# More block products by seven multiplications in the second SwiGLU of a streaming-encoder block

## The chip, the cores and the metric

The kernel runs on one core of a Trainium2 chip, as one launch. The metric is the device time of the whole launch in microseconds, the median over runs. Beside it stands one profiled execution, recorded by the hardware profiler; its span is the time from the first to the last recorded instruction.

## The reference

One residual block over 256 tokens of width 2048 in float32, with three sublayers, each followed by a layer norm:

```
x <- LN1(alpha*x + 1/2 * g1 * SwiGLU_1(mod1(x)))
x <- LN2(alpha*x +       g2 * W_out[ mLSTM(u) || RG-LRU(u) ])
x <- LN3(alpha*x + 1/2 * g3 * SwiGLU_2(mod3(x)))

def _swiglu(u, w13, w2):
    g, v = jnp.split(u @ w13, 2, axis=-1)
    return (jax.nn.silu(g) * v) @ w2
```

`mod(x)` is a layer norm without gain, times (1 + scale), plus shift. Shift, scale and gate of each sublayer are columns of `silu(c) @ w_ada + b_ada` (adaLN), a product of a 2048 x 18432 matrix with one vector. `w13` is 2048 x 11264 (gate columns, then value columns, 5632 each) and `w2` is 5632 x 2048. The change is in the third sublayer, SwiGLU_2.

## The kernel before

**Arithmetic.** A float32 weight tile of 128 x 2048 (1 MB) is loaded from DRAM into a `raw` buffer by a DMA of SyncE's queue. `split` (lines 101 to 111) turns it into two float32r tiles: ScalarE (ACT) casts it to `hi` (L108), and VectorE (DVE) subtracts to get `lo` (L110). A product is then three matmuls per 128 x 128 step: activation-high times hi, activation-high times lo, activation-low times hi. `mov_t` (L292 to L294 for work that the planner may move, L133 for work in the order written) does four such steps for one half t of the tokens: 12 matmuls of 128 x 512, called a block product here. `mov_w` does it for both token halves, 24 matmuls for one weight tile.

**The feed-forward stage.** The 5632 hidden columns are 11 blocks (0 to 10) of 512. A block needs eight `w13` tiles: gate and value columns, each with four row groups of 512 input rows. Block 0 begins inside the boundary of the sublayer before it. `rows_block` computes a block in the plain way: 8 tiles, 16 block products. `swiglu` multiplies silu(gate) by value, `turn_one` transposes the result on TensorE, and `w2` tiles multiply it, two blocks at a time, into four 512-column outputs `py`, which DVE adds to `yacc`.

**Seven products.** For blocks 2 to 9 (`FAST`), `fast_block` treats the first 1024 input rows as a 2 x 2 problem: two token halves by two row groups, times two row groups by gate and value columns. It takes seven block products in place of eight, from sums of activations (made once by `sums`, L688 to L703, and kept in `ws`, which takes the room of x) and from sums of weight tiles, made by DVE in place: `ta = tc - ta`, `ta = td - ta`, `tc = td - tc`, `tb = tb - ta` (L756, L761, L766, L775). Each sum is split like a loaded tile. The last 1024 rows (the second quad) are computed in the plain way, eight block products. Between the products stand four `w2` tiles of the two blocks before (`x_tile`).

**Order.** The framework has a planner: it lays the instructions out on each engine's in-order queue by a model of their durations, earlier program order first, and each instruction waits for the buffers and results that it needs. Work issued through the names T, V, A, G, Q keeps its written order. Tiles with one tag share a fixed number of buffers: four `raw`, three `hi`, three `lo`, two `row`, six `slot`, eight PSUM banks. A load waits in SyncE's queue until its buffer is free.

**adaLN tiles.** `tick`, called at each weight load, adds a rate to a credit, and for each whole credit an adaLN tile is loaded into a `raw` buffer too and multiplied and summed by DVE (L210). `FFN2_RATE` is 0.5 in the whole third sublayer, from a credit of -2.

**x.** `sums` stores x (2 MB) to DRAM (`xd`) by POOL's queue before its room is used. After block 9 `restore` loads it again, and ACT multiplies it by alpha. Then DVE multiplies `yacc` by the gate and adds it to x, eight pieces of 128 x 512 (L334, L335). Block 10 follows by `rows_block`, and `closing` does the `w2` products of blocks 8, 9 and 10 and the last layer norm.

Of the kernel before, what the change touches and what calls it, by code (L numbers as in the profile page):

```python
# [16 lines left out]
P = 128  # L17
D = 2048
# [23 lines left out]
FFN2_RATE = 0.5  # L42
# [3 lines left out]
FAST = range(2, 10)  # L46


class Held:
# [4 lines left out]
    def __getitem__(self, key):  # L54
        return self.tile[key]
# [3 lines left out]
def block_kernel(ctx: ExitStack, tc: tile.TileContext, a: dict, out: bass.AP):  # L59
# [594 lines left out]
    def ffn(s, w13, w2, start, following=None):  # L654
# [8 lines left out]
        b0 = RAMP // 4 if start else 0  # L663
# [5 lines left out]
        def rows_block(b, passed=None):  # L669

            i = 8 * (b - b0)
            if passed:
                pg, pv = passed[0], met(passed, w13[4:8], f"fv{s}")
            else:
                pg = [bank(f"fg{s}{b}{t}") for t in range(NT)]
                for k in range(4):
                    end = mov_w(pg, load_w(w13[i + k], f"fg{s}_{b}{k}"), uh, ul, k * 4, k == 0, k == 3)
                    if k in (1, 2):
                        turn_one(end)
                pv = [bank(f"fv{s}{b}{t}") for t in range(NT)]  # L680
                for k in range(4):
                    mov_w(pv, load_w(w13[i + 4 + k], f"fv{s}_{b}{k}"), uh, ul, k * 4, k == 0, k == 3)
# [5 lines left out]
        def sums():  # L688

            nc.gpsimd.dma_start(xd, x.tile)  # L690
            f = raw_tile("sums").rearrange("p (a b) -> p a b", b=P)
            for t in range(NT):
                tk = slice(t * P, (t + 1) * P)
                nc.vector.tensor_add(f[:, 8 * t:8 * t + 8, :], uh[:, 0:8, tk].bitcast(F32), ul[:, 0:8, tk].bitcast(F32))
            a11, a12, a21, a22 = (f[:, 4 * i:4 * i + 4, :] for i in range(4))
            nc.vector.tensor_add(a22, a21, a22)
            nc.vector.tensor_sub(a21, a11, a21)
            nc.vector.tensor_sub(a11, a22, a11)
            nc.vector.tensor_sub(a12, a12, a11)
            both = big.tile([P, 2, KT, P], F32R, tag="x", name="ws")  # L700
            nc.scalar.copy(both[:, 0], f)
            nc.vector.tensor_sub(both[:, 1], f, both[:, 0].bitcast(F32))
# [856 lines left out]
```

## Time and profile before

| | |
|---|---|
| median of 3 runs | 1883.22 us (1880.55 to 1883.65) |
| the profiled execution's own time | 1882.46 us |
| its span | 1880.7 us |
| TensorE busy | 1861.4 us, 99% of the span, 8495 matmuls |
| DVE busy | 1561.3 us, 83% |
| ACT busy | 895.1 us, 48% |
| POOL busy | 43.2 us, 2% |
| read from HBM, written | 514.46 MB, 4.22 MB |
| block 2's first product ends, block 9's first product ends | about 1246.6 us, about 1700.9 us |

A line of grouped instructions gives the kernel's line, the engine, the operation, what it writes and reads, the count, the busy time with the mean of one in nanoseconds, and the idle time ahead of it with what ended it. A timeline line gives start and duration in microseconds, then the instruction, and in brackets the engine's idle time before it and who ended it. Matmuls are pipelined: each shows some 390 ns, and what one costs is seen from the distance of their starts. POOL's queue is that of GpSimd.

### The profile page before, as it was taken

How to read it: one execution, taken by the hardware profiler on the slowest of the kernel's cores; microseconds unless marked ns; L12 is line 12 of the kernel's file. 1: busy time of each engine (PE TensorE's matmuls, PEld its weight loads, DVE VectorE, ACT ScalarE, POOL GpSimd, SP SyncE). 2: the span in 40 equal slices, each digit the busy share in tenths (PEclk: the TensorE clock that was granted, in tenths of full speed). 3: DMA queues.
4: the chain of work that ended last, by engine and by line, in shares of the span. 5: the costliest groups of instructions: out<-in, count | busy, mean ns of one | idle time of the engine just before them, and what ended most of it. 6: DMA issues, size and time to landing. Idle time of an engine off the chain costs nothing.

```text
span 1880.7 us, 21240 instructions
## 1 busy us (share of the span) xinstructions
PE 1861.4 (99%) x8495; PEld 1526.0 (81%) x8495; DVE 1561.3 (83%) x1467; ACT 895.1 (48%) x847; POOL 43.2 (2%) x68
## 2 busy tenths in 40 slices
PE   8999999999999999999999999999999999999998
PEld 5788888888888888788888887878778888888886
DVE  6899998887887987889997877789887788778776
ACT  4543444533334335756644356454544455545441
POOL 0000000000000000100000121000000000000000
PEclk9999999999999999999999999999999999999999
DMA  9989889999899987478687574768855654564662
GB/s 377 417 354 366 319 311 347 357 348 355 344 357 355 339 331 269 148 276 296 244 317 296 203 264 182 268 246 300 307 210 190 224 212 168 202 224 186 239 224 90
DMA packets 74931, 520.06 MB, mean 277 GB/s; under 512 B 8736, under 2 KB 8912, under 8 KB 13520
## 3 DMA queue, kind: packets, MB, share of 16 engines
q1 hardware_dynamic: 72144, 507.54, 71.6%
q0 software_dynamic: 960, 7.37, 1.0%
q10 hardware_dynamic: 1728, 3.80, 0.6%
q8 instruction: 66, 1.08, 0.2%
q14 instruction: 33, 0.27, 0.0%
HBM read 514.46 MB, written 4.22 MB: 276 GB/s over the span
## 4 chain that ended last, share of the span: by engine, by line
PE 92%; DVE 4%; DMA 2%; issue 1%; ACT 1%; POOL 0%; POOLq 0%; DVEq 0%; SPq 0%; ACTq 0%
PE py L133 9%; PE pj L281 5%; PE fa L133 5%; PE fb L133 4%; PE fc L133 3%; PE fd L133 3%; PE py L293 3%; PE py L294 3%; PE py L292 3%; PE pj L283 3%; PE fg L293 3%; PE fg L294 3%; PE fg L292 3%; PE fv L293 3%; PE fv L292 3%; PE fv L294 3%
## 5 line engine op out<-in xcount | busy, mean ns | idle before, releaser
L210 DVE CUSTOM_DVE_ANT_0 ada<-ada,scb,badac 128x2048 f32<-128x2048 f32 x110 | 258.0, 2345 | 39.5 <-DMA ada<-in_w_ada 39.0
L108 ACT CAST hw<-rw 128x2048 fp32r<-128x2048 f32 x81 | 155.1, 1914 | 218.0 <-DMA rw<-in_w 60.6
L110 DVE TENSOR_TENSOR lw<-rw,hw 128x2048 fp32r<-128x2048 f32 x81 | 185.1, 2287 | 55.8 <-ACT hw L108 55.0
L110 DVE TENSOR_TENSOR lfw<-rfw,hfw 128x2048 fp32r<-128x2048 f32 x48 | 109.9, 2289 | 17.2 <-ACT hfw L108 17.2
L281 PE MATMUL pj<-u,hs 128*128 128x512 f32 x512 | 122.5, 391 | 0.0
L108 ACT CAST hra<-rra 128x2048 fp32r<-128x2048 f32 x38 | 72.6, 1914 | 102.2 <-DMA rra<-in_w_r 43.1
L108 ACT CAST hfw<-rfw 128x2048 fp32r<-128x2048 f32 x48 | 91.9, 1915 | 47.8 <-PE py L133 28.2
L281 PEld LDWEIGHTS pj<-u,hs 128*128 128x128 f32 x512 | 94.3, 188 | 18.4
L133 PE MATMUL py<-lw,hth 128*128 128x512 f32 x256 | 99.8, 390 | 2.1 <-DVE lw L110 2.1
L133 PE MATMUL py<-hw,hth 128*128 128x512 f32 x256 | 100.4, 392 | 0.0
L293 PE MATMUL py<-lw,hth 128*128 128x512 f32 x256 | 99.8, 390 | 0.1
L294 PE MATMUL py<-hw,htl 128*128 128x512 f32 x256 | 99.7, 390 | 0.0
L133 PE MATMUL py<-hw,htl 128*128 128x512 f32 x256 | 99.7, 389 | 0.0
L292 PE MATMUL py<-hw,hth 128*128 128x512 f32 x256 | 97.3, 392 | 0.0
L108 ACT CAST hfg<-rfg 128x2048 fp32r<-128x2048 f32 x28 | 53.6, 1914 | 86.1 <-DMA rfg<-in_w 48.8
L108 ACT CAST hs<-rs 128x2048 fp32r<-128x2048 f32 x32 | 61.0, 1908 | 68.7 <-PE pj L281 53.6
L293 PE MATMUL fg<-lfg,u 128*128 128x512 f32 x224 | 87.4, 390 | 0.1
L294 PE MATMUL fg<-hfg,u 128*128 128x512 f32 x224 | 87.3, 390 | 0.0
L293 PE MATMUL fv<-lfv,u 128*128 128x512 f32 x224 | 87.2, 389 | 0.0
L294 PE MATMUL fv<-hfv,u 128*128 128x512 f32 x224 | 87.1, 389 | 0.0
L108 ACT CAST hfv<-rfv 128x2048 fp32r<-128x2048 f32 x28 | 53.6, 1913 | 66.7 <-DMA rfv<-in_w 41.3
L292 PE MATMUL fg<-hfg,u 128*128 128x512 f32 x224 | 84.5, 392 | 0.0
(727 smaller groups left out, 4764.4 us busy)
## 6 DMA issues: line engine op xcount, KB each, us to landing
ada<-in_w_ada SPq DMA_DIRECT2D x138, 1024.0 KB, 6.5
rw<-in_w SPq DMA_DIRECT2D x81, 1024.0 KB, 5.5
rfw<-in_w SPq DMA_DIRECT2D x50, 1024.0 KB, 4.8
rra<-in_w_r SPq DMA_DIRECT2D x45, 1024.0 KB, 7.4
rs<-in_w_s SPq DMA_DIRECT2D x32, 1024.0 KB, 5.0
rfg<-in_w SPq DMA_DIRECT2D x28, 1024.0 KB, 6.7
rfv<-in_w SPq DMA_DIRECT2D x28, 1024.0 KB, 5.5
rwo<-in_w_out SPq DMA_DIRECT2D x16, 1024.0 KB, 4.8
```

The lines of the kernel that those rows point to most:

```text
L108: act.copy(cut(hi, w), like(raw[:, w], hi))
L110: low.tensor_sub(cut(lo, w), like(raw[:, w], lo), cut(hi, w).bitcast(F32))
L133: self.last = getattr(self.engine, op)(*args, **kw)
L210: vec.tensor_tensor_reduce(raw[:, c], raw[:, c], scb[:, c], 1.0, base, ALU.mult, ALU.add, to)
L281: nc.tensor.matmul(ps, hi[:, k * P:(k + 1) * P], both(k), start=k == 0, stop=False)
L283: nc.tensor.matmul(ps[:, 0:S], lo[:, k * P:(k + 1) * P], uh[:, k, :], start=False, stop=k == KT - 1)
L292: pe.matmul(o, acth[:, k0 + j, tk], cut(hi, w), start=first and j == 0, stop=False, **kw)
L293: pe.matmul(o, acth[:, k0 + j, tk], cut(lo, w), start=False, stop=False, **kw)
L294: end = pe.matmul(o, actl[:, k0 + j, tk], cut(hi, w), start=False, stop=last and j == 3, **kw)
```

## The change

The third sublayer gets a function of its own, `last_ffn`. Block 0 and 1 are computed as before.

- Block 10 takes its first quad in seven products too. The `w2` products of blocks 8 and 9 with the first 512 output columns, which stood in `closing`, are placed inside it.
- Blocks 4, 6 and 8 (`DOUBLE`) take both quads in seven products each (plan `D6`); six `w2` tiles stand between them. The blocks after them (5, 7, 9) take one quad (plan `S2`), with two `w2` tiles. Blocks 2 and 3 keep the old order (`S4`).
- In blocks 4, 6, 8 two of the four weight sums of each quad are made by a DMA on POOL's queue that adds a weight tile from DRAM to the tile in SBUF: `c += d` and `a += b`. In other blocks DVE adds them. Signs are changed so that these are additions.
- The activation sums of the second quad are made once, at block 4, into one `slot` and one `row` buffer.
- x is multiplied by alpha and stored right after block 0. After block 9, DVE multiplies `yacc` by the gate in place, and a DMA on POOL's queue adds the stored x to it; `yacc` takes the place of x from there.
- The transposed result of a block lies in one `slot` buffer of its own, in place of two for two blocks. The row buffer for the tile `c` is no longer used.
- The adaLN rate is 0.8 per load in blocks 0 and 1 and 0.3 after, from a credit of 0; what is left is done at block 4.

```diff
-FFN2_RATE = 0.5
+FFN2_RATE = (0.8, 0.3)
...
-FAST = range(2, 10)
+DOUBLE = (4, 6, 8)
+BY_DMA = DOUBLE
...
+        def sums(q, to):
...
+            nc.vector.tensor_sub(a22, a21, a22)
+            nc.vector.tensor_sub(a21, a21, a11)
+            nc.vector.tensor_sub(a11, a22, a11)
+            nc.vector.tensor_add(a12, a12, a11)
+            hi, lo = to()
+            nc.scalar.copy(hi, f)
+            nc.vector.tensor_sub(lo, f, hi.bitcast(F32))
...
+            for w in plan:
...
+                if w == "P1":
+                    W["a", q] = fresh(q, 0, q == 0)
...
+                    end = part(at("1"), halves(W["a", q]), u, ku, 0, True, True)
+                    seen("1", "u", at("1"), q)
+                elif w == "P5":
+                    W["c", q] = fresh(q, 4, not DOUBLE and 4 <= b < n_b - 1)
+                    a, c = W["a", q], W["c", q]
+                    vec.tensor_sub(a[0], c[0], a[0])
+                    hl = halves(a, "p")
+                    if dma:
+                        nc.gpsimd.dma_start(c[0], w13[i + 2 * q + 5], accum_op=ALU.add)
+                    normal("5", hl, ws[q], 12, 0)
...
+                elif w == "P6":
+                    d = W["d", q] = fresh(q, 5, q == 1)
+                    vec.scalar_tensor_tensor(a[0], a[0], -1.0, d[0], op0=ALU.mult, op1=ALU.subtract)
+                    hl = halves(a, "q")
+                    if dma:
+                        nc.gpsimd.dma_start(a[0], w13[i + 2 * q + 1], accum_op=ALU.add)
+                    part(at("1"), hl, ws[q], 0, 0, False, True, True)
+                    seen("2", "gy", at("1"), q)
...
+                elif w == "P7":
+                    c = W["c", q]
+                    if not dma:
+                        vec.tensor_add(c[0], c[0], d[0])
+                    part(at("1"), halves(c, "q"), ws[q], 8, 0, False, True, True)
...
+                elif w == "P4":
+                    if not dma:
+                        vec.tensor_add(a[0], a[0], W["b", q][0])
+                    normal("4", halves(a, "r"), u, ku + 4, 1)
...
+        rows_block(0, nxt.pop())
+        scale_x()
+        nc.gpsimd.dma_start(xd, x.tile)
+        rows_block(1)
+        credit[1] = FFN2_RATE[1]
+        ws = [sums(0, in_x)]
+        S4 = "P1 t X t P5 X P6 P3 X P7 P2 G P4 G X V".split()
+        S2 = "P1 t G t P5 X P6 P3 G P7 P2 X P4 V".split()
+        D6 = "P1 t X t P5 X P6 P3 X P7 P2 P4 P1 X P5 X P6 P3 X P7 P2 P4".split()
+        for b in range(2, n_b - 1, 2):
+            kgs = (b - 2, b - 1)
+            if b == 4:
+                ada_until(s, 2, KT - 1)
+                if DOUBLE:
+                    ws.append(sums(1, in_slot))
+            if b in DOUBLE:
+                fast_block(b, ws, x_tiles(kgs, (0, 1, 2)), D6)
+                fast_block(b + 1, ws[:1], x_tiles(kgs, (3,)), S2)
+            else:
+                fast_block(b, ws[:1], x_tiles(kgs, (0, 1)), S4)
+                fast_block(b + 1, ws[:1], x_tiles(kgs, (2, 3)), S4)
+
+        gate_rows(s, 0.5)
+        for t in range(NT):
+            for n in range(4):
+                c = slice(n * 512, (n + 1) * 512)
+                nc.vector.tensor_mul(yacc[t][:, c], yacc[t][:, c], gate[:, c])
+            nc.gpsimd.dma_start(yacc[t], xd[:, t, :], accum_op=ALU.add)
+        x.tile = yacc
...
+        fast_block(n_b - 1, ws[:1], begun(), S2)
```

In a plan, P1 to P7 are the seven products of a quad, G one tile of the plain gate products, V the two tiles of the plain value products, X one `w2` tile, and t the transposes of the block before. `a` and `b` are the gate columns of the two row groups of a quad, `c` and `d` the value columns.

More of the change, by code (lines that the diff above doesn't have):

```diff
@@ L686, in rows_block @@
                 swiglu(b, t, pg[t], pv[t])
[L688 to L702, printed above, removed]
-            return both[:, 0], both[:, 1]
@@ L973, in g1 @@
             grp = groups[gi]
-            if start and gi == 2:
+            if gi == 2:
                 new_h(gi)
```

355 lines of the change are left out of this document (200 added, 155 removed).

## The prediction

> **What bounds the kernel now.** I read the page first, for shares and the chain of waits.
>
> ```profile
> span 1880.7 us, 21240 instructions
> PE 1861.4 (99%) x8495; PEld 1526.0 (81%) x8495; DVE 1561.3 (83%) x1467; ACT 895.1 (48%) x847; POOL 43.2 (2%) x68
> PE 92%; DVE 4%; DMA 2%; issue 1%; ACT 1%; POOL 0%; POOLq 0%; DVEq 0%; SPq 0%; ACTq 0%
> ```
>
> TensorE sets the end: 92% of the chain is its own work. So a matmul taken away is worth its spacing, as long as VectorE (DVE), at 83%, still delivers weights in time. The timeline of TensorE in block 2 gives that spacing and the price of a stall.
>
> ```profile
> 1251.43 0.60 PE L814 MATMUL th<-ident,sg 128*128 128x128 f32 x4
> 1251.78 0.47 PE L133 MATMUL fb<-hfw_20p,ws 128*128 128x512 f32 x1
> ...
> 1254.61 0.39 PE L133 MATMUL py<-hw,hth 128*128 128x512 f32 x1
> ...
> 1260.05 0.39 PE L133 MATMUL fa<-hfw_20q,ws 128*128 128x512 f32 x1
> 1263.02 0.50 PE L133 MATMUL fa<-lfw_20q,ws 128*128 128x512 f32 x1 [2.58 <-DVE lfw_20q L110]
> ...
> 1267.16 0.47 PE L133 MATMUL fb<-hfw,ws 128*128 128x512 f32 x1
> ```
>
> One `w2` tile, 24 matmuls, runs from 1254.61 to 1260.05: 5.44 us, 0.2267 us each, so a block product (12) is 2.72 us. Four transposes take 0.35 us. The stall was 2.58 us, and then 11 matmuls took 4.14 us (1263.02 to 1267.16) in place of 2.49: 1.65 us more at a lower clock. A stall of this length costs about 4.2 us.
>
> Next the copies of the first product, one in each of blocks 2 to 9, from the ScalarE (ACT) timeline:
>
> ```profile
> 1246.64 0.59 ACT L730 COPY fs<-fa 128x512 f32<-128x512 f32 x1
> 1314.89 0.59 ACT L730 COPY fs<-fa 128x512 f32<-128x512 f32 x1
> 1381.59 0.59 ACT L730 COPY fs<-fa 128x512 f32<-128x512 f32 x1
> 1446.92 0.59 ACT L730 COPY fs<-fa 128x512 f32<-128x512 f32 x1
> 1510.40 0.59 ACT L730 COPY fs<-fa 128x512 f32<-128x512 f32 x1
> 1573.90 0.58 ACT L730 COPY fs<-fa 128x512 f32<-128x512 f32 x1
> ```
>
> The last two intervals are 63.5 us, the undisturbed block (276 matmuls and 8 transposes, 62.57 + 0.70). The first three are 68.25, 66.70 and 65.33: blocks 2, 3 and 4 lose 4.8, 3.2 and 1.8 us. The windows and the DVE rows tell why:
>
> ```profile
> 300.00:600.00 300.00, 299.85 (x1339) 246.86 (x1338) 249.38 (x201) 123.44 (x87) 1.30 (x2) 1.00 0.93 354
> 1440.00:1700.00 260.00, 260.00 (x1167) 215.38 (x1166) 207.81 (x129) 135.45 (x95) 0.00 (x0) 1.00 0.54 196
> ```
> ```profile
> L210 DVE CUSTOM_DVE_ANT_0 ada<-ada,scb,badac x16: 2342/2350/2353, 1190.8 to 1363.5; 128x2048 f32<-128x2048 f32 x16
> ```
> ```profile
> 1258.40 2.35 DVE L210 CUSTOM_DVE_ANT_0 ada<-ada,scb,badac 128x2048 f32<-128x2048 f32 x1 [2.08 <-DMA ada<-in_w_ada]
> 1260.68 0.08 DVE L210 DVE_READ_ACCUMULATOR2_ANT adac<- 128x1 f32 x1
> 1260.68 2.29 DVE L110 TENSOR_TENSOR lfw_20q<-fw,hfw_20q 128x2048 fp32r<-128x2048 f32 x1
> 1262.88 2.28 DVE L110 TENSOR_TENSOR lfw<-rfw,hfw 128x2048 fp32r<-128x2048 f32 x1
> ```
>
> A window's columns are TensorE, weight loads, DVE, ACT, POOL, clock, DMA share, GB/s. From 1440 to 1700 TensorE is never idle with DVE at 207.81 of 260, 50.7 us a block. In blocks 2 and 3 come some 6 adaLN tiles each (12 of the 16), 2.28 us apart from the next start, 13.7 us: 64.4 us of DVE in a 63.5 us block, besides waits such as the 2.08 us for an adaLN tile's DMA, behind which the weight of the stalled product stood. A 128x2048 subtraction starts 2.20 us after the one before.
>
> **The change part by part**, against the profiled execution's own 1882.46 us (median of the three runs 1883.22, 0.76 above).
>
> (1) Products. Blocks 2 to 9 do 15 products today (7 for the first quad, 8 for the second) and block 10 does 16. Blocks 4, 6, 8 go to 14 (7 and 7), block 10 to 15; `w2` work only moves. Four products, 48 matmuls at 0.2267: **-10.9 us**.
>
> (2) adaLN rate. It is 0.8 per load in blocks 0 and 1 (11 loads, 8 tiles) and 0.3 after (24 loads, 8 tiles), so 4 in place of 6 in each of blocks 2 and 3: 50.7 + 4 x 2.28 = 59.8 us of DVE under 63.5. Of the 8.0 us those blocks lose, the part from overload goes; waits for a tile's DMA stay. I take 3 us left: **-5** (bounds 0 and -8). In blocks 0 and 1 a rate of 0.8 is covered by the window 300 to 600 above: FFN 1 runs at 0.88 per load there, 354 GB/s, and TensorE is idle 0.15 us of 300. So 0; the uncovered price is one stall, 4.2.
>
> (3) The second set of sums, made at block 4:
>
> ```profile
> 1216.21 2.35 DVE L694 TENSOR_TENSOR sums<-u 128x1024 f32<-128x1024 f32 x2
> 1218.59 0.69 DVE L696 TENSOR_TENSOR sums<-sums 128x512 f32<-128x512 f32 x1
> ...
> 1228.62 2.29 DVE L702 TENSOR_TENSOR ws<-sums,ws 128x2048 fp32r<-128x2048 f32 x1
> ```
>
> 2.35 + 4 x 0.69 + 2.29 = 7.4 us of DVE. Cover is the last step of block 3, the value products: 48 matmuls, 10.9 us, in which DVE has two splits (4.4) and some 2.4 us of small adds, 4.1 us free. 3.3 are left over. Today's block 4 pays 1.8 for the last adaLN tiles in the same place; I take 3 then, **+1.2** (-1.8 to +4.2).
>
> (4) DVE in a double block: 14 weight splits, 6 of `w2`, 4 sums, and 18 adds and multiplies of 512 columns at the row below.
>
> ```profile
> L745 DVE TENSOR_TENSOR yacc<-yacc,py 128x512 f32<-128x512 f32 x24 | 16.4, 683 | 6.5 <-PE py L133 6.5
> L108 ACT CAST hfw<-rfw 128x2048 fp32r<-128x2048 f32 x36 | 68.9, 1915 | 30.8 <-PE py L133 21.1 <-PE fd L133 4.0 <-PE fb L133 1.9
> ```
>
> 24 x 2.20 + 18 x 0.68 = 65.0 us, against 168 + 144 matmuls and 8 transposes on TensorE, 71.4 us: 91%. The single block beside it: 17 x 2.20 + 10 x 0.68 = 44.2 against 52.4, 84%. ACT's 20 casts make 38 us. So neither engine is the bound on average. Locally it is tighter: P7, P2, P4 and the next P1 follow each other with no `w2` tile between, 10.9 us of TensorE; in the second half DVE has 8.8 us of splits and six small operations, 12.9. It can be two weight tiles ahead, for `hi` and `lo` have three buffers (casts of that row wait for TensorE, 30.8 us), and so most of the 2.0 is hidden. I take 1 us for each of three, **+3**; the bounds are 0 and six stalls of 4.2, +25.
>
> (5) The sums by transfer. Twelve accumulating DMAs of 1 MB on POOL's queue, 4 a block; 12 MB in three blocks of 71.4 us add 56 GB/s to the 196 above. They spare DVE 12 x 2.20 us, which (4) has left out already. The trace has no accumulating DMA; the rows of POOL's queue, microseconds to landing at the end, bound it, with one plain load:
>
> ```profile
> rfw<-in_w SPq DMA_DIRECT2D x50, 1024.0 KB, 4.8
> gate<-rowd POOLq DMA_DIRECT2D x3, 1024.0 KB, 8.3
> xd<-x POOLq DMA_DIRECT2D x1, 2048.0 KB, 11.1
> x<-xd POOLq DMA_DIRECT2D x2, 1024.0 KB, 7.4
> ```
>
> From below 7.4; from above twice the 8.3, 16.6, if the old contents are fetched in a round of their own. I take 11.1, the row that moves 2 MB in one issue. What it may take: `a += b` can start when P6's split (a cast of 1.91 and a subtraction of 2.20) is done, at the latest as P6 starts, and is wanted by P4's cast, 4.1 us ahead of P4. From P6 to P4 lie P6, P3, a `w2` tile, P7 and P2: 4 x 2.72 + 5.44 = 16.3, less 4.1: **12.2 us**. `c += d` starts when `c - a` is done, 4.1 us ahead of P5, and is wanted 4.1 us ahead of P7, so it has P5, a tile, P6, P3, a tile: 19.0 us. So 11.1 fits: 0. Behind a late one stand P4's cast on ACT's queue, then its subtraction on DVE's, then all splits after, so TensorE's next products too. Bounds: 0 to six times (16.6 - 12.2 + 1.65), +36.
>
> The transfer could also start late, if POOL's issue and a DVE subtraction shut each other out. The nearest row:
>
> ```profile
> L708 POOL DMA_DIRECT2D x<-xd x2: 527/567/607, 1726.9 to 1727.6; - x2
> ```
> ```profile
> 1725.91 2.29 DVE L110 TENSOR_TENSOR lfw<-rfw,hfw 128x2048 fp32r<-128x2048 f32 x1 [0.82 <-ACT hfw L108]
> ```
>
> The issues at 1726.9 and 1727.6 fell into a DVE subtraction (1725.91 to 1728.20) and took 0.53 and 0.61 us, so I see no blocking. One whole subtraction of 2.29 us in front would make 11.1 into 13.4, late by 1.2 six times: +7.2. The Trainium skill (SBUF — State Buffer, Who interferes with whom) states such a lock, for a DVE operation with two SBUF inputs beside a GpSimd instruction that reads SBUF. This row doesn't show it.
>
> (6) The rest. `scale_x` (two ACT operations of 1.9 us) and the 2 MB store of x move ahead to block 1, where ACT idles some 3.5 us per weight tile behind TensorE:
>
> ```profile
> 1187.66 1.91 ACT L108 CAST hfg<-rfg 128x2048 fp32r<-128x2048 f32 x1 [3.56 <-PE fv2b L294]
> 1193.10 1.92 ACT L108 CAST hfg<-rfg 128x2048 fp32r<-128x2048 f32 x1 [3.53 <-PE fv2b L294]
> ```
>
> Each fits a gap: 0, or up to 4.2 where it doesn't. The store has POOL's queue alone and takes the 11.1 us of its row, from about 1196 to 1207; the first sums are written over x only around 1226 (their low half, L702 above, starts at 1228.62). After block 9 eight DVE adds (5.5 us) become two accumulating DMAs, wanted only in the closing, a block of 52 us later: 0. Block 10 gets three more splits and four sums on DVE (44.2 of 52.4 us) and the two `w2` tiles moved into it: 0, up to 4.2.
>
> Sum: -10.9 - 5 + 1.2 + 3 = **-11.7**: 1870.8 for the profiled execution, 1871.5 for the median. What this kernel's measurement can tell from no change is about 0.2%, 3.8 us.
>
> **Rivals.** *Nothing is lost in the double blocks*, and blocks 2 and 3 run clean: -10.9 - 8 = -18.9, 1864. For it, DVE's 91% and three buffers; against it, blocks 2 to 4 stalled at such loads.
>
> *DVE becomes the bound in the runs of four products.* The smaller stalls of today give the size (total, times, longest):
>
> ```profile
> PE py L133 <- DVE lw L110: 2.1, 2, 1.3
> ```
>
> Six of 1.3 us with 1.65 for the clock are 17.7 in place of 3: -10.9 - 5 + 1.2 + 17.7 = +3, 1886. With half of it, 1877. For it, the 12.9 against 10.9; against it, that only the second half is overloaded.
>
> *The accumulating transfer is late*, the case on the slow side: one place, the wait of P4's cast, in all six quads. It decides from 12.2 us to landing. At 14.2 it eats the forecast's gain (6 x 2.0 = 12.0); at 14.8 with the clock, 6 x (2.6 + 1.65) = 25.5, the result is 1897; at 16.6, 1908. For it: adaLN tiles already land later than the planner has placed their consumers (the 2.08 us above), and beside the new bytes the old ones must be fetched. Against it: 2 MB in 11.1 us.
>
> For the clock's part I go by the row: 2.58 us idle brought 1.65. The Trainium skill (TensorE: Matmul & The Clock Gate, Part 1) has the clock fall only after an idle window of about 3.4 us. The row doesn't agree; by the page the 14.8 case would cost 6 x 2.6 = 15.6 and end at 1887.
>
> *The gain doesn't come*, since raw tiles run short: in the second quad `a` and `c` hold two of the four for most of it. A buffer's round is 4.8 + 1.9 + 2.2 = 8.9 us, so two give a tile per 4.5 us, and four are wanted there in 7 x 2.72 + 3 x 5.44 = 35. Little speaks for it.
>
> **How the numbers follow.** Chances: the forecast 0.45 (1868 to 1878), the clean case 0.15, runs of products 0.17, late transfer 0.20, POOL's issue blocked 0.03 (1878.7). Bounds of no change are 1879.4 and 1887.0. The first two and the last are faster, 0.63, with 0.03 from the runs of products at half their price; 0.14 of these end within the bounds, as does 0.03 of the late transfer, the rest of which is slower, 0.17. So faster 0.66, within 0.17, slower 0.17. The range leaves out the late transfer above 1890 (0.14) and a tail of the clean case (0.04): 1863 to 1890.
>
> **What would show it.** (1) 48 fewer matmuls of 128x512. (2) First copies of blocks 2 and 3 nearer 63.5 us apart. (3) The pair 4 and 5 takes 123.8 us where two undisturbed blocks take 127. (4) TensorE's waits on `lo` tiles at P4 and P1 of 1 us or less. (5) The accumulating transfers' median landing under 12.2 us and no wait of ACT's P4 cast on DMA; a landing over 14 makes the prediction wrong on its sign. If TensorE waits in the double blocks for more than 11 us in all, the forecast fails too.

## The result, and the profile after

The changed kernel is slower: 1896.53 us median of 4 runs (1895.49 to 1897.79) beside 1881.88 us for the kernel before on the same chip, a ratio of 1.0072 with an interval of 1.0060 to 1.0084. The profiled execution took 1896.11 us, 13.65 more than that of before. The page of the changed kernel, its span, the engines' busy times and the shares of the chain of waits:

```profile
span 1894.3 us, 21297 instructions
PE 1858.6 (98%) x8447; PEld 1518.5 (80%) x8447; DVE 1605.1 (85%) x1498; ACT 921.1 (49%) x864; POOL 50.1 (3%) x80
PE 77%; DVE 11%; DMA 4%; issue 4%; ACT 4%; POOL 0%; POOLq 0%; DVEq 0%; SPq 0%; ACTq 0%
```

The matmuls fell by 48, from 8495 to 8447, as meant. But TensorE's share of the chain that sets the end fell from 92% to 77%, and DVE's rose from 4% to 11%: TensorE now waits for DVE. The list of TensorE's waits from 600 us on (total, times, longest) says at which operations:

```profile
PE th L970 <- DVE f L1149: 10.2, 4, 3.1
PE o L137 <- DVE tot L137: 3.7, 1, 3.7
...
PE f L137 <- DVE lfw_62q L114: 0.9, 1, 0.9
PE f L137 <- DVE lfw_42q L114: 0.9, 1, 0.9
PE f L137 <- DVE lfw_82q L114: 0.9, 1, 0.9
```

The kernel before had no wait of this length at either of the first two. TensorE's timeline gives their places; first the changed kernel's, and in the second fence the rows of the kernel before at the same marks:

```profile
764.60 1.85 PE L137 MATMUL o<-gate,tot 128*128 128x512 f32 x2 [3.65 <-DVE tot L137]
...
1155.59 0.50 PE L137 MATMUL f<-hf,u 128*128 128x512 f32 x1 [0.37 <-DVE u L137]
...
1252.54 0.60 PE L970 MATMUL th<-ident,sg 128*128 128x128 f32 x4
...
1383.58 0.60 PE L970 MATMUL th<-ident,f 128*128 128x128 f32 x4
...
1460.67 0.67 PE L970 MATMUL th<-ident,f 128*128 128x128 f32 x4 [3.06 <-DVE f L1149]
...
1514.93 0.60 PE L970 MATMUL th<-ident,f 128*128 128x128 f32 x4
...
1591.34 1.12 PE L970 MATMUL th<-ident,f 128*128 128x128 f32 x4 [3.06 <-DVE f L1149]
...
1645.40 0.60 PE L970 MATMUL th<-ident,f 128*128 128x128 f32 x4
...
1721.77 0.66 PE L970 MATMUL th<-ident,f 128*128 128x128 f32 x4 [3.06 <-DVE f L1149]
...
1756.10 0.50 PE L137 MATMUL py<-lw,ht 128*128 128x512 f32 x1 [1.57 <-DVE lw L114]
...
1777.78 0.60 PE L970 MATMUL th<-ident,f 128*128 128x128 f32 x4
```
```profile
1150.42 0.50 PE L133 MATMUL f<-hf,u 128*128 128x512 f32 x1 [0.37 <-DVE u L133]
...
1245.52 0.60 PE L814 MATMUL th<-ident,sg 128*128 128x128 f32 x4
...
1379.24 0.66 PE L814 MATMUL th<-ident,fs 128*128 128x128 f32 x4
...
1507.87 0.60 PE L814 MATMUL th<-ident,fs 128*128 128x128 f32 x4
...
1634.86 0.60 PE L814 MATMUL th<-ident,fs 128*128 128x128 f32 x4
```

The rows `th` without a wait are the first transposes that run in blocks 2, 4, 6, 8 and 10, just behind P1: marks that stand at the same place of a block in both kernels (block 10 aside). The row `f` at 1155.59 stands at the start of the third sublayer. Between marks:

| stretch | before | after | difference |
|---|---|---|---|
| up to the third sublayer (`f`) | 1150.42 | 1155.59 | +5.2 |
| from there to block 2's mark | 95.10 | 96.95 | +1.9 |
| blocks 2 and 3 | 133.72 | 131.04 | -2.7 |
| blocks 4 and 5 | 128.63 | 131.35 | +2.7 |
| blocks 6 and 7 | 126.99 | 130.47 | +3.5 |
| from block 8's mark to the end of the span | 245.84 | 248.90 | +3.1 |

So there are two losses. One of 5.2 us lies ahead of the sublayer that the prediction was about. The other lies in the pairs with a double block: 131.4 and 130.5 us, and 132.4 for blocks 8 and 9 (1645.40 to 1777.78), where 123.8 and a little was predicted.

**The first loss** comes from a part of the change that neither the prediction nor the description of the change tells of: the diff also drops a line, `credit[:] = 0.0, 0.0`, ahead of the last `w2` products of the first sublayer (`g2_kept`). Without it the adaLN rate of that sublayer goes on, and DVE multiplies seven more tiles between 685 and 728 us, ahead of the boundary; TensorE's `o` at 764.60 waits 3.65 us for DVE. In the last sublayer ten tiles are then left in place of sixteen (the second has one fewer); the last of the ten starts at 1252.13, at block 2's mark. The windows from 700 to 800 us (columns as in the prediction), after and before, show DVE busy 85.1 us in place of 76.5 and TensorE idle 4.0 us in place of 0.6:

```profile
700.00:800.00 100.00, 95.97 (x412) 74.22 (x411) 85.11 (x128) 58.98 (x110) 6.39 (x12) 0.98 0.68 264
```
```profile
700.00:800.00 100.00, 99.37 (x435) 77.72 (x434) 76.45 (x121) 63.04 (x114) 6.40 (x12) 1.00 0.56 208
```

**The second loss**, at 1460.67: DVE's rows around the end of block 4, and ACT's row with them:

```profile
1454.33 0.68 DVE L1144 TENSOR_TENSOR f<-f,f 128x512 f32<-128x512 f32 x1
1454.93 2.28 DVE L1087 TENSOR_TENSOR fw<-rfw,fw 128x2048 f32<-128x2048 f32 x1
1457.13 2.28 DVE L114 TENSOR_TENSOR lfw<-rfw,hfw 128x2048 fp32r<-128x2048 f32 x1
1459.33 0.68 DVE L1144 TENSOR_TENSOR f<-f,f 128x512 f32<-128x512 f32 x1
1459.93 0.68 DVE L1149 TENSOR_TENSOR f<-f,f 128x512 f32<-128x512 f32 x1
```
```profile
1455.04 0.64 ACT L1145 ACTIVATE f<-f 128x512 f32<-128x512 f32 x1 [0.92 <-DVE f L1144]
```

The silu of the first token half is done at 1455.68. Its multiplication (L1149), which the transposes need, starts only at 1459.93: ahead of it in DVE's in-order queue stand the next block's sum `c - a` (L1087), a split and the second half's addition. DVE has no pause here; from 1440 to 1470 it is busy 28.8 us of 30. That the place in the queue makes this wait is argued here, and tested by e16_order2 below.

### The profile page after: what moved, and what is told of

Its sections match the earlier page's. It is cut to its first block, busy times and chain, and to the rows that moved or that the text cites. A ratio compares the mean times of both kernels' runs of the same rounds, so it can differ in the third digit from the quotient of the medians.

```text
span 1894.3 us, 21297 instructions
## 1 busy us (share of the span) xinstructions
PE 1858.6 (98%) x8447; PEld 1518.5 (80%) x8447; DVE 1605.1 (85%) x1498; ACT 921.1 (49%) x864; POOL 50.1 (3%) x80
## 3 DMA queue, kind: packets, MB, share of 16 engines
q8 instruction: 66, 1.08, 0.2%
## 4 chain that ended last, share of the span: by engine, by line
PE 77%; DVE 11%; DMA 4%; issue 4%; ACT 4%; POOL 0%; POOLq 0%; DVEq 0%; SPq 0%; ACTq 0%
PE f L137 15%; PE py L137 7%; PE pj L285 5%; PE pj L287 3%; PE py L297 3%; PE py L298 3%; PE py L296 3%; PE fg L297 2%; PE fg L298 2%; PE fv L296 2%; PE fv L297 2%; PE fv L298 2%; PE rv L760 2%; PE fg L296 2%; PE rv L761 2%
## 5 line engine op out<-in xcount | busy, mean ns | idle before, releaser
L214 DVE CUSTOM_DVE_ANT_0 ada<-ada,scb,badac 128x2048 f32<-128x2048 f32 x110 | 258.2, 2347 | 13.0 <-DMA ada<-in_w_ada 12.9
L137 PE MATMUL f<-hfw,u 128*128 128x512 f32 x576 | 185.3, 393 | 0.0
L137 PE MATMUL py<-hw,ht 128*128 128x512 f32 x512 | 163.4, 390 | 0.0
L137 PEld LDWEIGHTS f<-hfw,u 128*128 128x128 f32 x576 | 109.5, 190 | 22.9
L137 PE MATMUL f<-lfw,u 128*128 128x512 f32 x288 | 113.3, 393 | 0.3 <-DVE lfw L114 0.3
L137 PEld LDWEIGHTS py<-hw,ht 128*128 128x128 f32 x512 | 96.1, 188 | 19.8
L137 PE MATMUL py<-lw,ht 128*128 128x512 f32 x256 | 99.8, 390 | 2.4 <-DVE lw L114 2.4
L297 PE MATMUL py<-lw,hth 128*128 128x512 f32 x256 | 99.8, 390 | 0.1
L298 PE MATMUL py<-hw,htl 128*128 128x512 f32 x256 | 99.7, 390 | 0.0
L296 PE MATMUL py<-hw,hth 128*128 128x512 f32 x256 | 97.3, 392 | 0.0
L137 DVE CUSTOM_DVE_ANT_0 ada<-ada,scb,badac 128x2048 f32<-128x2048 f32 (+1 forms) x34 | 73.5, 2160 | 4.2 <-DMA ada<-in_w_ada 4.0
```

The source lines that it names most:

```text
L137: self.last = getattr(self.engine, op)(*args, **kw)
L214: vec.tensor_tensor_reduce(raw[:, c], raw[:, c], scb[:, c], 1.0, base, ALU.mult, ALU.add, to)
L296: pe.matmul(o, acth[:, k0 + j, tk], cut(hi, w), start=first and j == 0, stop=False, **kw)
L297: pe.matmul(o, acth[:, k0 + j, tk], cut(lo, w), start=False, stop=False, **kw)
L298: end = pe.matmul(o, actl[:, k0 + j, tk], cut(hi, w), start=False, stop=last and j == 3, **kw)
```

## The experiments

All ratios are to the kernel before on the same chip. "Pairs" are blocks 4+5, 6+7, 8+9 between the same marks as above; two undisturbed blocks of before take 127.0. The runs were made on several chips, so ratios are compared and not times.

| kernel | ratio (interval) | pairs, us |
|---|---|---|
| the change | 1.0072 (1.0060-1.0084) | 131.4, 130.5, 132.4 |
| e1_credit | 1.0045 (1.0029-1.0062) | 131.3, 130.7, 132.0 |
| b1_noreset | 1.0006 (0.9997-1.0016) | |
| e2_turn | 1.0057 (1.0042-1.0072) | |
| e3_both | 1.0024 (1.0015-1.0033) | 130.4, 129.3, - |
| e8_p2 | 1.0023 (1.0012-1.0033) | |
| e4_nodma | 1.0177 (1.0162-1.0193) | 138.4, 132.5, 137.2 |
| e7_alldma | 1.0060 (1.0043-1.0077) | |
| e10_gate | 1.0052 (1.0036-1.0069) | |
| e5_single | **0.9974 (0.9965-0.9984)** | 127.0, 127.0, 127.1 |
| e11_single_gate | 0.9987 (0.9977-0.9996) | |
| e12_nosums2 | 1.0064 (1.0047-1.0082) | 130.1, 129.2, 139.8 |
| e13_noyacc | 1.0043 (1.0026-1.0059) | 130.3, 130.9, 131.4 |
| b2_rate | 1.0005 (0.9996-1.0014) | |
| e16_order2 | 1.0055 (1.0042-1.0067) | 132.5, 131.4, 131.4 |
| e17_order3 | 1.0080 (1.0066-1.0093) | 132.6, 131.8, 131.8 |
| e18_dma5_7 | 1.0021 (1.0012-1.0030) | 129.2, 128.0, 131.5 |
| e19_dma5_9 | 1.0009 (1.0000-1.0018) | 129.2, 128.0, 130.3 |

**e1_credit**: the change with the dropped line put back.

```diff
             if gi == len(groups) - 1:
+                credit[:] = 0.0, 0.0
                 g2_kept(gi - 1)
```

> The changed kernel with one line put back: the adaLN credit is set to 0 before the last w2 products of the FIRST feed-forward stage, as in the kernel before. Theory (the stall at the first boundary comes from adaLN tiles that now run ahead of it): TensorE's wait of 3.7 us on DVE's totals at 765 us goes, the second sublayer starts some 5 us earlier; 6 or 7 adaLN tiles come back into blocks 0 to 3 of the last stage and cost 0 to 3 there; about 1891 to 1894 us, the three stalls of 3.06 us after blocks 4, 6, 8 stay. Rival (the boundary's stall has nothing to do with adaLN tiles): the wait stays, 1896.

1.0045: some 5 us come back, and in its trace the third sublayer starts 4.5 us earlier. The wait of `o` is 0.3 us there, and the four waits of the transposes stay at 10.2. In the changed kernel the line is the cause of the first loss.

**b1_noreset**: the kernel before without that line.

```diff
-                credit[:] = 0.0, 0.0
                 g2_kept(gi - 1)
```

> The kernel BEFORE with that one credit line taken out, nothing else. Theory: the first boundary alone costs 5 us, of which the last stage gives back up to 4 since 6 adaLN tiles fewer run in blocks 2 and 3, where they stall it: 1883 to 1887 us, with a wait of some 3.7 us on DVE's totals at 765 us. Rival (the boundary's stall belongs to the rest of the change): no such wait there, 1878 to 1882.

There the line is worth nothing that can be told from no change, though TensorE waits 3.0 us at the boundary too. The profiled execution doesn't show where that comes back: it is the slowest of the ten (1888.75 us; the fastest took 1881.87), its third sublayer starts 6.8 us later, and of these only 1.6 return, in blocks 4 and 5. Blocks 2 and 3 take 134.8 us, no less than before.

**e2_turn and e3_both**: the transposes of a double block one gate tile later; e3_both has it on top of e1_credit.

```diff
-        S2 = "P1 t G t P5 X P6 P3 G P7 P2 X P4 V".split()
+        S2 = "P1 G t P5 X t P6 P3 G P7 P2 X P4 V".split()
```

> The changed kernel with the plan S2 (blocks 5, 7, 9, 10) as 'P1 G t P5 X t P6 ...' in place of 'P1 t G t P5 X P6 ...': the transposes of the block before come one and three steps later. Theory (what was lost is the wait of the first transposes for the last adds, silu and multiply of a double block, 3.06 us three times, with the clock's fall behind it): those waits go, each with 1.6 us of clock, -14 to -15 us, about 1882 us, double block to double block near 126 us in place of 131. Rival (DVE is the bound at the end of a double block, the transposes only show it): the wait moves to the weight tiles of P5 or P6, the time stays above 1891.

> Both edits: credit put back and transposes later. Theory: the two losses add, 1875 to 1879 us, below the kernel before (about 1882). Rival (DVE-bound with the adaLN tiles back in the stage): 1885 or more.

The waits for the transposes are gone, and in their place TensorE waits for weight tiles behind the double blocks: six times, 7.5 us in all, 1.6 at the longest, in both kernels. (In e2_turn a wait of 3.2 us for a `w2` tile in block 9 comes on top.) Most of the stall moves to the next thing that DVE makes: e3_both is 4 us below e1_credit, where 14 to 15 were expected from the transposes.

**e8_p2**: e3_both with another product ahead of P6 in the second quad.

```diff
-... P1 X P5 X P6 P3 X P7 P2 P4".split()
+... P1 X P5 X P2 P6 P3 X P7 P4".split()
```

> The kernel with credit put back and transposes later, and in the second quad of blocks 4, 6, 8 the product P2 moved ahead of P6, so that the end is P7, P4 in place of P7, P2, P4 and P6's weight has 2.7 us more. Theory (DVE is late because four products follow each other, and P6's chain of sums is too short by 0.87 us): the P6 wait goes (1.5 us with the clock, three times) and the wait after the block shrinks: 4 to 9 us less than the kernel with both edits. Rival (DVE's total in the double block is the bound, any order gives the same): within 2 us.

Again moved: the wait at P6 (0.87) is gone, the waits behind the double block grow to 2.0, and the time is the same.

**e4_nodma**: the change with all sums on DVE.

```diff
-BY_DMA = DOUBLE
+BY_DMA = ()
```

> The changed kernel with BY_DMA = (): the two sums of each quad in blocks 4, 6, 8 go back to DVE, four subtractions of 2.2 us a block. Theory (DVE is what TensorE waits for at the end of a double block): 8.8 us more DVE in a block that already stalls, most of it on the path, 5 to 9 us a block, 1910 to 1922 us. Rival (transfers spare nothing, their landing is what is waited for): 1896 or less.

About 20 us more than the change. Twelve DVE sums of 2.2 us are 26.4, and by the traces the three pairs take 13.9 us more, so about half of each microsecond of DVE work added to a double block is a microsecond of the kernel. Besides the transposes TensorE waits there for `w2` tiles and for splits at P5 and P6, up to 2.65 us. Another 5.3 us lie behind block 10's mark, where these sums don't stand: TensorE waits 3.3 us there, behind a weight load for which DVE stood 3.87.

**e7_alldma, e10_gate**: e3_both with the sums of all seven-product blocks by transfer; then of blocks 4 to 10, with the gate row's transfers ahead of block 9. **e9_alldma_p2** (e7 with e8's order) was expected to add the gains of both, 0.994 to 0.998, and came out at 1.0062 (1.0047-1.0077), no better than e7_alldma, with a wait of 8.1 us for the `w2` tile of block 9.

```diff
-BY_DMA = DOUBLE
+BY_DMA = range(2, 11)      # e10_gate: range(4, 11), and gate_rows(s, 0.5) ahead of block 9
```

> The kernel with credit put back and transposes later, and in blocks 2 to 10 all (not only 4, 6, 8) the sums c+d and a+b made by transfer: two DVE operations of 2.2 us fewer in each of blocks 2, 3, 5, 7, 9, 10, no product more or less. Theory (DVE's backlog at the start of a single block, where c+d now stands ahead of the split that TensorE wants): the waits of 1.62 and 0.87 us after blocks 4, 6, 8 go with their clock loss, 3 us each, and some of block 2's, 5 to 10 us in all below the kernel with both edits. Rival (fixed latencies of the chain split, sum, cast, split, not DVE's load): the same waits, within 2 us of that kernel.

> The kernel with credit put back and transposes later, sums c+d and a+b by transfer in blocks 4 to 10, and the loading of the gate row (its transpose, the two small transfers) moved ahead of block 9. Theory (DVE stands still for the gate row's landing, 4 to 8 us ahead of its multiplications of yacc, and TensorE then waits for a w2 tile): the 7.5 us wait that all sums by transfer had in block 9 goes and the waits after blocks 4 and 6 are a half of those with both edits, 1879 to 1885 us, ratio 0.998 to 1.001. Rival (the landing is late wherever the load stands): a wait of 4 us or more on a w2 tile in block 9 stays, 1888 or more.

The waits of 0.87 in the blocks behind the double ones went (those of 1.63 stayed), but another came: counted from block 8's mark, DVE reaches the multiplications by the gate 2.0 us sooner than in e3_both, the gate row lands 3.1 us later, and DVE stands there for it. In e7_alldma:

```profile
1747.97 3.70 DVE L1180 TENSOR_TENSOR yacc<-yacc,gate 128x512 f32<-128x512 f32 x6 [8.39 <-DMA gate<-rowd]
```

TensorE waits 7.5 us behind it. In e10_gate the wait of the same length moved to P4 of block 8 (`lfw_82r`, 7.5): the multiplications by the gate now stand ahead of that split in DVE's queue, and DVE waits there for the gate row, whose transfer was issued at 1695.59:

```profile
1704.76 3.70 DVE L1183 TENSOR_TENSOR yacc<-yacc,gate 128x512 f32<-128x512 f32 x6 [6.46 <-DMA gate<-rowd]
1708.38 2.29 DVE L114 TENSOR_TENSOR lfw_82r<-rfw,hfw_82r 128x2048 fp32r<-128x2048 f32 x1
```

**e5_single and e11_single_gate**: e1_credit without double blocks, and with the gate row's transfers ahead of block 9.

```diff
-DOUBLE = (4, 6, 8)
+DOUBLE = ()
```

> The changed kernel with the adaLN credit put back and DOUBLE = (): no block takes both quads in seven products, so no accumulating weight sums and no second set of activation sums; block 10 keeps its seven products and x is added from DRAM. Theory (the double blocks lose more in waits than the three products they save): without them the kernel is faster than with them, 1878 to 1884 on a chip where the kernel before takes 1883, against 1891 with them (credit put back alone). Rival (the loss lies in block 10, the gate and the adding of x): it stays above 1887.

> The kernel without double blocks (credit put back, DOUBLE = ()) and with the gate row's load moved ahead of block 9, where the tile c of block 9 goes to a raw buffer. Theory: a product fewer (2.7 us), blocks 2 and 3 with fewer adaLN tiles (3 to 5 us) and no wait for the gate: 1874 to 1879 where the kernel before takes 1883, ratio 0.995 to 0.998. Rival (block 10 with sums is DVE-bound like the double blocks): 1882 or more.

e5_single beats both kernels: 1879.57 us against 1883.81, 0.26% less. (Without double blocks the tile `c` of blocks 4 to 9 goes to a row buffer again, as before.) Its window from 1380 to 1700, and in the second fence that of the change:

```profile
1380.00:1700.00 320.00, 320.00 (x1433) 265.01 (x1432) 253.98 (x158) 165.67 (x118) 0.00 (x0) 1.00 0.54 200
```
```profile
1380.00:1700.00 320.00, 310.92 (x1368) 254.32 (x1367) 267.64 (x168) 174.46 (x121) 10.35 (x12) 0.99 0.69 224
```

TensorE is never idle without the double blocks. With them it is idle 9.1 us in this stretch, and its clock falls behind the two longest waits (see the last section). The double blocks cost 0.0071 of the time, 13.4 us (1.0045 less 0.9974), though they save 8.2 us of products. The gate row ahead of block 9 was no gain (a wait of 2.1 us for a `w2` tile).

**e12_nosums2, e13_noyacc**: is the 3.06 us wait set by the amount of DVE work in the second quad?

```diff
+                    if q == 0:                                 # e12: both sums of the second quad
                         vec.tensor_sub(a[0], c[0], a[0])
...
-                    else:
+                    elif kgs[0] + 2 not in DOUBLE or n == 3:   # e13
                         nc.vector.tensor_add(yacc[t][:, c], yacc[t][:, c], pss[t])
```

> This leaves out, from the kernel of e1_credit, DVE's two sums (c - a and -a - d) of the second quad in blocks 4, 6 and 8, so its output is not the reference's. That is 2 x 2.2 = 4.4 us of DVE work less in each double block. Theory (the amount of DVE work in the second quad sets both waits): the wait of the first transposes, 3.06 us, goes below 1 us and so does the wait at P6 of 0.9, so with the clock some 3 to 4.5 us a block come back: 9 to 13 us, a ratio of 0.9975 to 0.9995. Rival (a fixed chain of add, silu and multiplication at the block's end, whatever the amount of work before it): only the wait at P6 goes, 0.9 to 1.5 a block, 2.7 to 4.5 us in all, a ratio near 1.0025, and the transposes still wait about 3 us.

> This leaves out, from the kernel of e1_credit, DVE's adds to yacc for three of the four 512-column parts in the steps of the double blocks, so its output is not the reference's. That is 3.7 us of DVE work less in a double block, none of it a link of the chain that leads to the transposes. Theory (amount of DVE work): the 3.06 us waits shrink to about 1 or less, 8 to 11 us in all, a ratio of 0.9985 to 1.0005. Rival (fixed chain): the waits stay at about 3 us, at most 2 us in all come back, a ratio of 1.0035 to 1.0045.

No. With 4.4 or 3.7 us of DVE work less the wait at P6 went (0.3 at most is left), and the other stayed at 3.05 to 3.06 us in all three blocks. e12_nosums2, TensorE:

```profile
1455.56 1.00 PE L971 MATMUL th<-ident,f 128*128 128x128 f32 x4 [3.05 <-DVE f L1152]
```

The rival held as far as the wait goes. DVE cannot bank what it saves earlier: the split for P4 waits 1.19 us for its cast in e12_nosums2 and in e1_credit alike (2.38 in e13_noyacc), so DVE comes to the same queue of work at the same point of TensorE's. The cast in turn waits for TensorE. In the change, as in e1_credit and e12_nosums2, ACT idles 3.52 us ahead of P4's cast in all six quads, until the `w2` product before P7 is done, whose `hi` buffer is the one of three that comes free next:

```profile
1446.77 1.92 ACT L112 CAST hfw_42r<-rfw 128x2048 fp32r<-128x2048 f32 x1 [3.52 <-PE py L137]
```

The time of e12_nosums2 is no better than e1_credit's because of a gate row wait: TensorE stands 8.09 us for a `w2` tile in block 9, as in e7_alldma.

**e16_order2**: the same work in another order: the multiplication ahead of `c - a`, and the next block's `c + d` behind the split for P5.

```diff
+                        with behind():                         # DVE: behind the first multiplication
                             vec.tensor_add(f[to], f[to], at(key))
...
+                    with behind(quads == 1):
                         vec.tensor_sub(a[0], c[0], a[0])
...
+                        with behind(True, split_p):            # DVE: behind the split for P5
                             vec.tensor_add(c[0], c[0], d[0])
```

> The kernel of e1_credit with another order on DVE's queue where a double block ends, and the same work: the first multiplication of the double block goes ahead of its last addition and ahead of the next block's sum c - a, and the next block's sum c + d goes behind the split for P5. Theory (the place of c - a in the queue makes the wait): the four waits of the transposes, 10.2 us in all, go below 1 us in all, and with about 2 us of clock each three times some 13 us come back, less up to 2 us for a P5 split that is now late: 1878 to 1881, a ratio of 0.9965 to 0.9985. Rival (DVE has too much work around the end of the double block, in whatever order): the wait moves to the next split, P5's or the w2 tile's, with 2 us or more, and the ratio stays between 1.001 and 1.0045.

The transposes wait 0.8 us in all in place of 10.2, so the place in the queue did set that wait. Yet the time is no better than e1_credit's. The next splits are late now (waits of TensorE, total, times, longest):

```profile
PE py L137 <- DVE lw L114: 5.0, 4, 1.4
PE f L137 <- DVE lfw L114: 3.4, 4, 0.9
PE f L137 <- DVE lfw_70q L1042: 1.4, 1, 1.4
PE f L137 <- DVE lfw_50q L1042: 1.4, 1, 1.4
PE f L137 <- DVE lfw_90q L1042: 1.3, 1, 1.3
...
PE th L971 <- DVE f L1167: 0.8, 3, 0.3
```

**e17_order3**: besides, the second quad's `yacc` additions behind the split for P5, and the multiplications by the gate moved into block 10.

> e16_order2, and besides in the double blocks' second quad the additions to yacc go behind the split for P5, and after block 9 the multiplications of yacc by the gate go behind splits of block 10 (two each behind those of P6, P3, P7, P2) in place of into block 9, where they waited for the gate row. Theory: the waits of 0.85 us at the second P6 shrink below 0.4 (with the clock 3 us in all) and no wait for the gate row is left (about 1): 1874 to 1878, 0.995 to 0.997. Rival (total DVE work bounds these places): the P6 waits stay at 0.8 or move to the w2 tile behind it, and block 10 waits in place of block 9: no better than e16_order2.

The theory was wrong on both counts: the waits at the second P6 grew to 1.4, and a weight load in block 10 that landed late (DVE stood 5.08 us for it) cost TensorE 3.1.

**e18_dma5_7 and e19_dma5_9**: e16_order2 with `c + d` and `a + b` by transfer in the single blocks behind double ones, two of them and all three; in e19_dma5_9 the multiplications by the gate also go behind the split for block 9's P4.

```diff
-BY_DMA = DOUBLE
+BY_DMA = range(4, 9)       # e19_dma5_9: range(4, 10)
```

> e16_order2 with the sums c + d and a + b of blocks 5 and 7 by transfer too (block 9's stay on DVE): 2.2 us of DVE work less between the splits for P5 and for the w2 tile, 2.2 more later. Theory (the DVE work in the stretch right behind a double block sets the waits): in blocks 5 and 7 the waits of 1.39 (w2 tile), 1.38 (P6) and 0.87 (gate tile) go below 0.4 each, in block 9 they stay; with the clock some 4 to 5 us come back in each of two blocks, 8 to 10 in all: 1884 to 1886, a ratio of 1.000 to 1.0015. Rival (the chain sum, cast, split between P5 and P6 sets them, whatever stands around it): the P6 waits stay at 1 us or more and the ratio stays above 1.003.

> e18 with block 9's sums by transfer as well, and the multiplications of yacc by the gate behind the split for block 9's P4, so that they don't wait for the gate row (7.5 us in the kernel of e7_alldma). Theory: three blocks gain 4 to 5 us against e16_order2 and no gate wait comes up: 1879 to 1882, a ratio of 0.997 to 0.999, about that of e5_single. Rival (as for e18, or the gate row's wait only moves on): above 1.002.

In blocks 5 and 7 the waits for the `w2` tile and for the gate tile (1.4 and 0.9) are gone, and in block 9 of e18_dma5_7 they are still there. So the DVE work in that stretch sets these. The P6 waits only went from 1.4 to 0.76 to 0.88, neither below the theory's 0.4 nor at the rival's 1 or more; what is left has the rival's cause, since DVE stands still there while ACT casts between the sum and the split. e19_dma5_9:

```profile
1463.15 2.28 DVE L1115 SCALAR_TENSOR_TENSOR fw<-fw,rfw 128x2048 f32<-128x2048 f32 x1
1467.46 2.29 DVE L1042 TENSOR_TENSOR lfw_50q<-fw,hfw_50q 128x2048 fp32r<-128x2048 f32 x1 [2.03 <-ACT hfw_50q L112]
```

By the ratios 6.4 and 8.7 us came back against e16_order2, where 8 to 10 and 12 to 15 were expected, and neither reaches e5_single.

**b2_rate**: the kernel before with the adaLN rates alone.

```diff
-            credit[:] = -2.0, FFN2_RATE
+            credit[:] = 0.0, 0.8
...
+            credit[1] = 0.3       # after block 1
```

> The kernel before with the adaLN rates alone: 0.8 per load in blocks 0 and 1 from a credit of zero, 0.3 from block 2 on. Theory (the prediction's second term): blocks 2 and 3 lose 3 us instead of 8.0, so -5, a ratio of 0.9973; what the changed kernel showed in those blocks (a wait of 1.14, one of 1.14, one of 0.83 in block 2, none in block 3) agrees with about -4, 0.998. Rival (the tiles put into blocks 0 and 1 stall those blocks instead): a stall there of about 4.2 us, a ratio of 1.000.

No gain. DVE's rows of this kernel show why: an adaLN tile stands in front of other work while its load is on the way, in the boundary ahead of block 0 and again in block 2.

```profile
1172.96 2.35 DVE L210 CUSTOM_DVE_ANT_0 ada<-ada,scb,badac 128x2048 f32<-128x2048 f32 x1 [2.12 <-DMA ada<-in_w_ada]
...
1269.74 2.35 DVE L210 CUSTOM_DVE_ANT_0 ada<-ada,scb,badac 128x2048 f32<-128x2048 f32 x1 [4.95 <-DMA ada<-in_w_ada]
```

TensorE waits 1.28 us at 1175.72 behind the first and 3.30 us at 1274.35 behind the second, and in block 2 another 2.09 at 1259.84 for a `w2` tile. In blocks 2 and 3 it takes 135.0 us, more than the 133.7 of before; e1_credit, with as many tiles starting in them (three and three), takes 131.5. What else in the changed blocks lets the tiles come in time wasn't tried.

## Why the prediction was wrong

The prediction said -11.7 us for the profiled execution; it was +13.65. Term by term, an undisturbed pair being 127.0 - 2.7 = 124.3 us with one product less:

| step of the prediction | predicted | measured |
|---|---|---|
| (1) products | -10.9 | -10.9 (48 matmuls) |
| (2) adaLN rate | -5 | -0.8 (+1.9 ahead of block 2, -2.7 in blocks 2 and 3) |
| (3) second sums, block 4 | +1.2 | -0.9 (0.7 lost there in place of 1.6) |
| (4) DVE in double blocks | +3 | about +19 |
| (5) accumulating transfers | 0 | 0 |
| (6) the rest | 0 | +1.6 (gate row in block 9) |
| not in the prediction: the dropped line | - | +5.2 |

These add up to +13.2; 0.4 is not placed. (4) is what the three pairs take over 124.3 (7.1, 6.2, 8.1), less the 0.7 and 1.6 that stand in other rows. Row (2) is the change as it stands, with no adaLN tile left behind block 2's mark; with the dropped line back and sixteen tiles (e1_credit) the same stretches give +2.0 and -2.2.

**Step (4) failed, and it decided the sign.** Its average was right (DVE was busy 109.0 us in blocks 6 and 7, where 65.0 and 44.2 had been counted), and so was its suspicion of the run P7, P2, P4, P1: 12.9 us of DVE against 10.9. Two things in it were not. It ended the run at P1, though behind it the next block's sums and splits follow at once: in the change and in e16_order2 DVE's work from the split for P4 to the split for the next block's P3 is seven splits, three sums and eight small operations, 7 x 2.2 + 3 x 2.2 + 8 x 0.6 = 26.8 us, against nine products and eight transposes on TensorE, 9 x 2.72 + 0.7 = 25.2. And it held that two tiles of lead hide most of the 2.0 us. The three buffers do allow two tiles and no more: P4's cast stood 3.52 us for a buffer, and in e12_nosums2 work taken out before P4 did not shorten the wait by 0.1 us. On top stood a place in the queue that no sum over durations shows: a multiplication needed at once, behind a 2.2 us sum needed later. So "1 us for each of three" became some 6 us for each. 3.06 of it is the wait of the first transposes; behind it come 1.7 and 1.5 us at a lower clock in the first two, and in the third, where the clock stayed, a second wait of 1.08.

The forecast's own signs said so: (2) block 2 took 67.5 us and only block 3 the 63.5, (3) pairs of 123.8 (they took 130 to 132), (4) waits on `lo` tiles of 1 us or less at P4 and P1 (true there, but the wait came at the transposes behind them, which the prediction did not name). The waits came to 2.9 us in the double blocks and 10.2 at the transposes right behind them, over the 11 us of the last sign only if both are counted.

**The rival with DVE as the bound in runs of four products** (0.17, 1886) had the engine right, and for its price of 17.7 us 19 was measured. That the two agree is partly luck: it had six stalls of 1.3 us with a clock loss behind each, and there were three of 3.06 at a place that it didn't name, with shorter ones around them. It came out 10 us too low because of the dropped line, step (2) and the gate row.

**Step (2) was mis-sized, and part of its premise was false.** It put the 8.0 us that blocks 2 and 3 lose down to 12 adaLN tiles. Between the copies that it used as marks the rows of before show ten, the last at 1363.46, so block 4's 1.8 us, which step (3) put down to such tiles, isn't theirs either. And in the changed kernel, with none behind block 2's mark, the two blocks still take 4.0 us more than 127.0, all of it in block 2, where TensorE waits 3.1 us in all for the activation sums (`ws`) and two splits. So 2.7 of the 5 came, the higher rate that was costed at 0 in blocks 0 and 1 took 1.9 back, and b2_rate shows no gain at all from the rate alone. The "uncovered price, one stall" was the better figure.

**Step (5) was right**, and the rival with the late transfer (0.20, the largest) false; that its 1897 us lies next to the measured 1896.5 is chance. The changed kernel's transfers on POOL's queue, with microseconds to landing at the end:

```profile
rfw<-in_w POOLq DMA_DIRECT2D x9, 1024.0 KB, 8.2
...
gate<-rowd POOLq DMA_DIRECT2D x3, 1024.0 KB, 8.0
...
fw<-in_w POOLq DMA_DIRECT2D x3, 1024.0 KB, 8.6
...
yacc<-xd POOLq DMA_DIRECT2D x2, 1024.0 KB, 11.6
```

The twelve sums land in 8.2 and 8.6 us (medians of nine and three) where 11.1 was taken and 12.2 was the budget, and no cast for P4 waits for a DMA. Nothing shows POOL's issue held back by DVE. e4_nodma adds that they were worth 14 us to the three pairs. The rival of short raw tiles doesn't show either: from 1383 to 1780 us one cast of ACT waits for a load, 1.35 us at 1764.95, and DVE waits for none but the gate row.

**Step (6)** held but for the gate row: one wait of DVE for its landing (4.24 us at 1751.94), which became TensorE's 1.57 us at 1756.10. That wait grew to 8.4 us in e7_alldma and 9.0 in e12_nosums2, where DVE came to it sooner and the row landed no sooner.

**The dropped line** was in the diff and was read over. Nothing in the working could make up for it: the list of parts was made from the third sublayer alone.

## What to carry to other kernels

Where one engine feeds another through two or three buffers, its share over a block says little: write down its queue over the densest stretch, on through the start of the next block, and compare that with the consumer's time there. Here a stretch with 1.6 us more work for DVE than for TensorE went with a loss of some 6 us a pair, and the product saved was worth 2.7. And read every hunk of a diff for its stage before pricing any: a line outside the part that the change is about cost 5 us here.

## What the runs showed of the hardware

An accumulating DMA of 1 MB from DRAM into SBUF landed in 8.2 to 8.6 us (medians), 0.2 to 0.6 later than a plain one on the same queue (`gate`, one row of 8 KB spread over the partitions, 8.0); its issue took longer on POOL, 0.86 us against 0.57, by the groups of POOL from 1380 to 1760 us:

```profile
L1100 POOL DMA_DIRECT2D fw<-in_w x3 | 2.6, 857 | 43.8 <-DVE lfw_60q L114 16.0 <-DVE lfw_80q L114 16.0 <-DVE lfw_40q L114 11.8
...
L238 POOL DMA_DIRECT2D gate<-rowd x1 | 0.6, 571 | 3.1 <-PE f L137 3.1
```

The Trainium skill (DMA: Bandwidth & Descriptors, Anatomy of one DMA) fits 2.0 us plus the bytes at 436 GB/s, an estimate of 4.4 us for 1 MB on GpSimd's queue; no row of that queue here agrees, with 224 GB/s moved at the same time.

A wait of 3.06 us could lower the clock, but did not always. Of the change's three such waits two did: the granted clock was 0.53 from 1461.0 to 1464.5 and 0.62 from 1591.6 to 1595.2, but 1.00 from 1722.1 to 1725.6, behind the third. The ten matmuls behind the first, from the change's timeline:

```profile
1461.08 0.69 PE L137 MATMUL f<-hfw,u 128*128 128x512 f32 x1
1461.56 0.63 PE L137 MATMUL f<-lfw,u 128*128 128x512 f32 x1
...
1465.05 0.39 PE L137 MATMUL f<-lfw,u 128*128 128x512 f32 x1
```

They take 3.97 us, where ten at 0.2267 take 2.27: 1.7 us lost. The Trainium skill (TensorE: Matmul & The Clock Gate, Part 1) wants an idle window of about 3.4 us for this, so the first two waits disagree with it, as the 2.58 us of before did.
